# Folding the adaLN partial sums to 64 partitions, with the high part above the low part, before one matmul with ones

## The chip, the cores and the metric

The kernel runs on one core of one Trainium2 chip. The metric is device time in microseconds (us) of one execution. The profile that is read below was taken of one such execution.

## The reference

Two layers of a decoder trunk, 256 tokens wide 1024. Each layer has three sublayers (feed-forward, attention, feed-forward); layer 0's attention is sparse, layer 1's is differential. Every sublayer is wrapped in norms and in a shift, a scale and a gate that come from a conditioning vector `c`:

```
cond = silu(c)
mod = cond @ ada_w[i] + ada_b[i]            # 1024 x 9216 per layer
sh0, sc0, g0, sh1, sc1, g1, sh2, sc2, g2 = split(mod, 9)
h = rmsnorm(x, pre_norm) * (1 + sc) + sh
x = x + (0.5 or 1) * g * rmsnorm(sublayer(h), post_norm)
```

The change is about the 1024-wide pieces of `mod`. All data are float32.

## The kernel before

**Main work.** The two row tiles of x (128 tokens each, t = 0 and 1) go through the six sublayers n = 0 to 5 as two generators that a loop takes turns with. Every weight block is loaded by a DMA on SP's queue into a `raw` tile, then split into a high and a low part: ScalarE (ACT) casts the high part (lines 211 and 234), VectorE (DVE) subtracts it from the raw values to get the low part (lines 212 and 235). TensorE (PE) multiplies high by high, high by low and low by high (lines 267 and 282). Split weights are called `whl` or `wj`; seven such tiles exist. `raw` tiles come from a pool of five buffers, temporary tiles (`tmp`) from a pool of four.

**The modulation vectors.** One piece of `mod` is one call of `ada_items`. Each of the sixteen pieces (all but the shift and scale of sublayer 0, which `first_part` makes) has four items. An item loads 1 MB of `ada_w` (line 307) and adds two products of it into a 128 x 1024 tile `a` with two VectorE instructions (line 311); row p of `a` then holds the partial sum over the eight rows of `ada_w` that lie on partition p. After the fourth item, `end()` adds the 128 partitions up and spreads the sum to all of them: ACT casts `a` to the high part (line 320), DVE subtracts for the low part (line 321), and PE multiplies each half of each part by a matrix of ones (lines 326 and 327: four matmuls of 512 columns, with two in each accumulation). The result `ps_m` is then copied by ACT if the piece is a shift (`sh`, line 329) or combined with a norm weight by DVE if it is a scale or a gate (`g`, `pg`, lines 331 and 333). The norm weight `pnb` is loaded by line 319.

**Order.** `background()` hands out items as the main work goes on, by the table BGCUM: twenty items, so five ends, fall into sublayer 0, and one to four ends into each later one. The ends are called place 1 to place 16 here, in order of time; places 1 to 5 lie between 107 and 221 us, place 6 at 298 us in the sparse attention, place 14 starts at 712 us and is finished in the norm ahead of the differential attention at 735 us. Within an engine the order is laid down by a scheduler when the program is built, and an instruction that waits holds up everything behind it on its engine.

Of the kernel before, what the change touches and what calls it, by code (L numbers as in the profile page):

```python
# [8 lines left out]
F32 = mybir.dt.float32  # L9
F32R = mybir.dt.float32r  # L10
I32 = mybir.dt.int32
AF = mybir.ActivationFunctionType
OP = mybir.AluOpType
# [31 lines left out]
def bcast_rows(ap, n):  # L45
    return bass.AP(tensor=ap.tensor, offset=ap.offset, ap=[[0, 128], [1, n]])
# [3 lines left out]
def trunk(ctx, tc, x, c, positions, ada_w, ada_b, pre_norm, post_norm, ffn_w_gate, ffn_w_up,  # L50
          ffn_w_down, dsa_w_in, dsa_w_out, diff_w_in, diff_w_out, diff_lambda, diff_subln, out):
    nc = tc.nc
    consts = ctx.enter_context(tc.tile_pool(name="consts", bufs=1))
    wpool = ctx.enter_context(tc.tile_pool(name="wpool", bufs=WBUFS))
    rawp = ctx.enter_context(tc.tile_pool(name="rawp", bufs=RAWBUFS))
# [8 lines left out]
    def tmp(name, shape=(128, 1024), dt=F32):  # L64
        return tmpp.tile(list(shape), dt, name=name, tag="tmp")
# [7 lines left out]
    def tr_tile(name):  # L73
        return psum.tile([128, 4, 128], F32, name=name, tag="tr", bufs=2)
# [4 lines left out]
    def half(hf):  # L79
        return slice(hf * 512, (hf + 1) * 512)  # L80

    def flat(t):
        return t.rearrange("p a b -> p (a b)")
# [22 lines left out]
    onesr = consts.tile([128, 128], F32R, name="onesr")  # L106
# [182 lines left out]
    def mod_tile(n, name):  # L289
        MOD.setdefault(n, {})[name] = t = consts.tile([128, D], F32, name=name, tag="mod", bufs=MODBUFS)  # L290
        return t

    def ada_items(n, part):


        l, s = divmod(n, 3)
        c0 = (3 * s + part) * D
        box = {}

        def begin():  # L300
            box["a"] = a = mod_tile(n, ("sh", "g", "pg")[part])
            nc.gpsimd.memset(a, 0.0)
            nc.sync.dma_start(a[0:1, :], ada_b[l:l + 1, c0:c0 + 1024])

        def go(i):
            raw = rawp.tile([128, 2, 1024], F32, name="araw", tag="raw")
            nc.sync.dma_start(raw, ada_w[l, :, c0:c0 + 1024].rearrange("(p j) n -> p j n", j=8)[:, 2 * i:2 * i + 2, :])
            a = box["a"]
            with tc.high_priority(offset=APRI):
                for j in range(2):  # L310
                    nc.vector.scalar_tensor_tensor(a, raw[:, j, :], scond[:, 2 * i + j:2 * i + j + 1], a,  # L311
                                                   op0=OP.mult, op1=OP.add)

        def end():
            a = box["a"]
            hl = rawp.tile([128, 2, 1024], F32R, name="ahl", tag="raw")
            if part:
                pb = tmp("pnb")
                nc.sync.dma_start(pb, bcast_rows((post_norm if part == 2 else pre_norm)[l, s], D))
            nc.scalar.copy(hl[:, 0, :], a)  # L320
            nc.vector.tensor_tensor(hl[:, 1, :], a, hl[:, 0, :].bitcast(F32), op=OP.subtract)
            m = a
            for hf in range(2):
                sl = half(hf)
                ps = tr_tile("ps_m")
                nc.tensor.matmul(flat(ps), onesr, hl[:, 0, sl], start=True, stop=False)
                nc.tensor.matmul(flat(ps), onesr, hl[:, 1, sl], start=False, stop=True)
                if part == 0:
                    nc.scalar.copy(m[:, sl], flat(ps))
                elif part == 1:  # L330
                    nc.vector.scalar_tensor_tensor(m[:, sl], flat(ps), 1.0, pb[:, sl], op0=OP.add, op1=OP.mult)
                else:
                    nc.vector.scalar_tensor_tensor(m[:, sl], flat(ps), 1.0 if s == 1 else 0.5, pb[:, sl],
                                                   op0=OP.mult, op1=OP.mult)

        def item(i):
            if i == 0:
                begin()
            go(i)
            if i == 3:  # L340
                end()

        return [lambda i=i: item(i) for i in range(4)]
# [645 lines left out]
```

## Time and profile before

| | us |
|---|---|
| median of three runs (1059.56 to 1062.03) | 1059.62 |
| the profiled execution's own time | 1058.01 |
| its span in the trace | 1056.2 |
| PE busy in the span | 1015.5 |
| DVE busy | 788.6 |
| ACT busy | 523.8 |

Matmuls overlap one another, so PE's busy time says that it has work, and the distance between two starts says what one matmul takes. [...]

### The profile page before, as it was taken

What the parts mean: (1) busy time and instruction counts of PE and PEld (TensorE: products, weight loads), DVE (VectorE), ACT (ScalarE), POOL (GpSimd) and SP (SyncE); (2) the same over time, 40 slices, a digit from 0 to 9 for tenths busy, and PEclk for the clock granted to TensorE, in tenths of its full rate; (3) what the DMA queues carried; (4) which work ended last, traced back from release to release, by engine and by line L of the source; (5) the groups of instructions that cost most, each with busy time, mean ns of one, the idle gap of its engine ahead of it and who ended that gap; (6) DMA issues with size and microseconds to landing.
All of it is one profiled execution on the core that took longest, in us unless ns stands there. A gap on an engine that the chain in (4) does not pass through costs nothing.

```text
span 1056.2 us, 15311 instructions
## 1 busy us (share of the span) xinstructions
PE 1015.5 (96%) x5936; PEld 873.6 (83%) x5936; DVE 788.6 (75%) x1121; ACT 523.8 (50%) x834; POOL 45.0 (4%) x49
## 2 busy tenths in 40 slices
PE   5999999989999999999999999999999899999997
PEld 2689997769778789998878999887777678999875
DVE  5769887989976977877688967767988575765643
ACT  3354534455575654543455544346477555544432
POOL 1000000001000200000030000001000120000000
PEclk9999999999999999999999999999999999999999
DMA  9959899986443477988757979956653443778431
GB/s 315 343 147 322 313 321 378 347 293 218 148 142 128 155 273 247 352 286 291 271 193 260 314 257 316 316 208 236 260 200 118 153 134 115 243 235 261 183 117 40
DMA packets 93732, 249.48 MB, mean 236 GB/s; under 512 B 6084, under 2 KB 24652, under 8 KB 93660
## 3 DMA queue, kind: packets, MB, share of 16 engines
q1 hardware_dynamic: 93660, 248.52, 68.1%
q8 instruction: 46, 0.75, 0.3%
q14 instruction: 26, 0.21, 0.1%
HBM read 247.44 MB, written 1.05 MB: 235 GB/s over the span
## 4 chain that ended last, share of the span: by engine, by line
PE 57%; issue 20%; DVE 4%; ACT 3%; POOL 2%; DMA 1%; POOLq 0%; DVEq 0%; ACTq 0%
PE ydown L267 15%; PE up L282 9%; PE gate L282 8%; PE gate L267 3%; PE up L267 3%; PE projQd L267 2%; PE projQ L267 2%; PE projV L267 2%; PE projA L267 2%; PE projK L267 2%; PE ydsa L267 1%; POOL rstd L407 1%; DVE whl L235 1%; PE dsaO L752 1%; PE ydiff L267 1%
## 5 line engine op out<-in xcount | busy, mean ns | idle before, releaser
L235 DVE TENSOR_TENSOR whl<-raw,whl 128x1024 fp32r<-128x1024 f32 (+3 forms) x216 | 245.7, 1150 | 98.5 <-ACT whl L234 97.7
L234 ACT CAST whl<-raw 128x1024 fp32r<-128x1024 f32 (+3 forms) x216 | 211.8, 995 | 190.1 <-PE ydown L267 89.5
L282 PE MATMUL gate<-HT,wj 128*128 128x256 f32 x1344 | 166.2, 284 | 1.5 <-DVE wj L212 1.4
L212 DVE TENSOR_TENSOR wj<-raw,wj 128x1024 fp32r<-128x1024 f32 x112 | 134.7, 1221 | 43.1 <-ACT wj L211 42.8
L211 ACT CAST wj<-raw 128x1024 fp32r<-128x1024 f32 x112 | 116.4, 1050 | 100.3 <-DMA raw<-in_ffn_w_up_dram 21.5
L282 PEld LDWEIGHTS gate<-HT,wj 128*128 128x128 f32 x1344 | 163.4, 192 | 2.2 <-DVE wj L212 1.9
L282 PE MATMUL up<-HT,wj 128*128 128x256 f32 x1344 | 164.4, 283 | 0.0
L282 PEld LDWEIGHTS up<-HT,wj 128*128 128x128 f32 x1344 | 162.8, 192 | 0.4
L267 PE MATMUL ydown<-whl,ffj 128*128 128x512 f32 x672 | 157.0, 390 | 2.2 <-DVE whl L235 2.2
L267 PEld LDWEIGHTS ydown<-whl,ffj 128*128 128x128 f32 x672 | 125.7, 188 | 30.6 <-DVE whl L235 3.1
L267 PE MATMUL gate<-whl,HT 128*128 128x480 f32 x384 | 94.3, 392 | 0.4 <-ACT HT L393 0.2
L267 PE MATMUL ydown<-whl,ffa 128*128 128x512 f32 (+1 forms) x368 | 89.3, 393 | 1.9 <-ACT whl L234 1.9
L267 PEld LDWEIGHTS gate<-whl,HT 128*128 128x128 f32 x384 | 72.2, 191 | 16.6 <-ACT HT L393 2.7
L267 PEld LDWEIGHTS ydown<-whl,ffa 128*128 128x128 f32 (+1 forms) x368 | 67.9, 188 | 19.7 <-issue 3.6
L311 DVE SCALAR_TENSOR_TENSOR pg<-araw,scond,pg 128x1024 f32<-128x1024 f32 x48 | 61.4, 1280 | 6.4 <-DMA araw<-in_ada_w_dram 5.8
L267 PE MATMUL up<-whl,HT 128*128 128x480 f32 x288 | 66.0, 381 | 0.0
L267 PEld LDWEIGHTS up<-whl,HT 128*128 128x128 f32 x288 | 53.5, 188 | 8.4 <-ACT sg L512 0.5
L311 DVE SCALAR_TENSOR_TENSOR g<-araw,scond,g 128x1024 f32<-128x1024 f32 x40 | 51.2, 1281 | 7.8 <-DMA araw<-in_ada_w_dram 7.4
L311 DVE SCALAR_TENSOR_TENSOR sh<-araw,scond,sh 128x1024 f32<-128x1024 f32 x40 | 51.2, 1280 | 1.3 <-DMA araw<-in_ada_w_dram 0.8
L468 POOL TENSOR_TENSOR rstdy<-rstdy,mhalf 128x1 f32<-128x1 f32 x12 | 10.2, 850 | 824.2 <-ACT rstdy L467 824.2
L267 PE MATMUL projV<-whl,HT 128*128 128x512 f32 x96 | 28.4, 416 | 0.0
L267 PE MATMUL projQ<-whl,HT 128*128 128x512 f32 x96 | 27.6, 415 | 0.0
(224 smaller groups left out, 1090.7 us busy)
## 6 DMA issues: line engine op xcount, KB each, us to landing
araw<-in_ada_w_dram SPq DMA_DIRECT2D x64, 1024.0 KB
raw<-in_ffn_w_down_dram SPq DMA_DIRECT2D x40, 1024.0 KB
raw<-in_ffn_w_gate_dram SPq DMA_DIRECT2D x56, 512.0 KB
raw<-in_ffn_w_up_dram SPq DMA_DIRECT2D x56, 512.0 KB
raw<-in_ffn_w_gate_dram SPq DMA_DIRECT2D x16, 960.0 KB
raw<-in_diff_w_in_dram SPq DMA_DIRECT2D x12, 1024.0 KB
raw<-in_ffn_w_up_dram SPq DMA_DIRECT2D x12, 960.0 KB
fraw<-in_ada_w_dram SPq DMA_DIRECT2D x32, 256.0 KB
```

Of the source, the lines that this page charges most:

```text
L211: nc.scalar.copy(hl[0], raw)
L212: nc.vector.tensor_tensor(hl[1], raw, hl[0].bitcast(F32), op=OP.subtract)
L234: nc.scalar.copy(hl[:, 0, 0:n], raw[:, j, 0:n])
L235: nc.vector.tensor_tensor(hl[0:r, 1, 0:n], raw[0:r, j, 0:n], hl[0:r, 0, 0:n].bitcast(F32), op=OP.subtract)
L267: nc.tensor.matmul(acc[:, hf, 0:n], lhs, rhs, start=(first and hf not in seen), stop=(last and i % 3 == 2))
L282: nc.tensor.matmul(a[:, b, :], w[:, wp, j, b * 128:(b + 1) * 128], HT[:, :, hp, k0 + j, :], start=(first and j == 0 and i == 0 and b % 2 = ...
L311: nc.vector.scalar_tensor_tensor(a, raw[:, j, :], scond[:, 2 * i + j:2 * i + j + 1], a, op0=OP.mult, op1=OP.add)
L407: nc.gpsimd.tensor_tensor(r, r, mhalf[:, 0:1], op=OP.pow)
L468: nc.gpsimd.tensor_tensor(r, r, mhalf[:, 0:1], op=OP.pow)
L752: nc.tensor.matmul(flat(O)[:, h * 64:(h + 1) * 64], ptb[u][:, i * nb + b, :], v[:, b, :], start=(b == 0), stop=(b == nb - 1), skip_group_c ...
```

## The change

In `end()`, ACT first copies rows 64 to 127 of `a` down to partitions 0 to 63 of a new tile `aup`, and DVE adds rows 0 to 63 to them. The sum of 64 rows is then split: ACT casts it to the high part on partitions 0 to 63 of `ahl`, DVE writes the low part to partitions 64 to 127. One matmul of ones over all 128 partitions then adds high and low at once, so each half takes one matmul in place of two. `aup` lies in the `raw` pool where `ahl` lay before, and `ahl` moves to the `tmp` pool. The load of `pnb` now stands behind the allocation of both tiles.

```diff
         def end():
             a = box["a"]
-            hl = rawp.tile([128, 2, 1024], F32R, name="ahl", tag="raw")
+            up = rawp.tile([128, 2, 1024], F32, name="aup", tag="raw")
+            hl = tmp("ahl", (128, 1024), F32R)
             if part:
                 pb = tmp("pnb")
                 nc.sync.dma_start(pb, bcast_rows((post_norm if part == 2 else pre_norm)[l, s], D))
-            nc.scalar.copy(hl[:, 0, :], a)
-            nc.vector.tensor_tensor(hl[:, 1, :], a, hl[:, 0, :].bitcast(F32), op=OP.subtract)
+            w, f = up[0:64, 0, :], up[0:64, 1, :]
+            nc.scalar.copy(w, a[64:128, :])
+            nc.vector.tensor_tensor(f, a[0:64, :], w, op=OP.add)
+            nc.scalar.copy(hl[0:64, :], f)
+            nc.vector.tensor_tensor(hl[64:128, :], f, hl[0:64, :].bitcast(F32), op=OP.subtract)
             m = a
             for hf in range(2):
                 sl = half(hf)
                 ps = tr_tile("ps_m")
-                nc.tensor.matmul(flat(ps), onesr, hl[:, 0, sl], start=True, stop=False)
-                nc.tensor.matmul(flat(ps), onesr, hl[:, 1, sl], start=False, stop=True)
+                nc.tensor.matmul(flat(ps), onesr, hl[:, sl], start=True, stop=True)
```

Lines 320 and 321 thus become four: 323 (ACT copy), 324 (DVE add), 325 (ACT cast) and 326 (DVE subtract); the matmul is line 331, and every line of the program behind it is 4 higher than before (the cast of a weight stays line 234, the copy of a shift is 333).

The scheduler also lays the order down anew. At place 3, in the down projection of sublayer 0, ACT's order was this (`ahl<-sh` is the high part of the shift's sums, `whl<-raw` the high parts of weights):

```order
L234 CAST whl<-raw 128x1024 x2
L393 CAST ffj<-actj 128x512
L320 CAST ahl<-sh 128x1024
L329 COPY sh<-ps_m 128x512 x2
L234 CAST whl<-raw 128x1024 x8
```

and is now this:

```order
L234 CAST whl<-raw 128x1024 x2
L397 CAST ffj<-actj 128x512
L323 COPY aup<-sh 64x1024
L325 CAST ahl<-aup 64x1024
L333 COPY sh<-ps_m 128x512 x2
L234 CAST whl<-raw 128x1024 x8
```

Both of ACT's steps and the copies of the result stand ahead of the next eight casts of weights.

At place 4, one piece later, DVE's order was this (line 311 makes the partial sums, line 333 the result, line 235 the low parts of weights):

```order
L235 TENSOR_TENSOR whl<-raw,whl 128x1024 x2
L311 SCALAR_TENSOR_TENSOR pg<-araw,scond,pg 128x1024 x2
L321 TENSOR_TENSOR ahl<-pg,ahl 128x1024
L333 SCALAR_TENSOR_TENSOR pg<-ps_m,pnb 128x512 x2
L235 TENSOR_TENSOR whl<-raw,whl 128x1024 x2
```

and is now this:

```order
L235 TENSOR_TENSOR whl<-raw,whl 128x1024 x2
L311 SCALAR_TENSOR_TENSOR pg<-araw,scond,pg 128x1024 x2
L324 TENSOR_TENSOR aup<-pg,aup 64x1024
L326 TENSOR_TENSOR ahl<-aup,ahl 64x1024
L337 SCALAR_TENSOR_TENSOR pg<-ps_m,pnb 128x512 x2
L235 TENSOR_TENSOR whl<-raw,whl 128x1024 x2
```

The add and the subtraction stand one behind the other, with nothing between them for the time in which ACT casts; place 5 reads the same.

At place 14 the subtraction has moved. It stood 20 microseconds ahead of the norm; DVE's order in the norm of t = 0 ahead of the differential attention was this (`h` is the modulated row tile, `HT` the low part of its transpose):

```order
L235 TENSOR_TENSOR whl<-raw,whl 128x1024
L415 SCALAR_TENSOR_TENSOR h<-h,rstd,sh 128x512 x2
L235 TENSOR_TENSOR whl<-raw,whl 128x1024
L394 TENSOR_TENSOR HT<-ps_x,HT 128x512 x2
L470 TENSOR_TENSOR u<-ydown,pg 128x512 x2
```

and is now this:

```order
L235 TENSOR_TENSOR whl<-raw,whl 128x1024
L419 SCALAR_TENSOR_TENSOR h<-h,rstd,sh 128x512 x2
L235 TENSOR_TENSOR whl<-raw,whl 128x1024
L326 TENSOR_TENSOR ahl<-aup,ahl 64x1024
L398 TENSOR_TENSOR HT<-ps_x,HT 128x512 x2
L474 TENSOR_TENSOR u<-ydown,pg 128x512 x2
```

The subtraction now stands between the weights and `HT`.

## Rows read from the trace of the kernel before

**Rows 1.** The page: busy us (share of the span), instructions.
```profile
PE 1015.5 (96%) x5936; PEld 873.6 (83%) x5936; DVE 788.6 (75%) x1121; ACT 523.8 (50%) x834; POOL 45.0 (4%) x49
```
**Rows 2.** Stretches: length, PE, PEld, DVE, ACT, POOL busy (instructions), PE clock, DMA share, GB/s.
```profile
100.00:150.00 50.00, 49.89 (x409) 49.34 (x408) 43.96 (x48) 20.32 (x23) 0.00 (x0) 1.00 0.85 305
...
175.00:200.00 25.00, 24.12 (x104) 18.94 (x103) 23.00 (x21) 10.26 (x11) 0.00 (x0) 1.00 1.00 362
...
600.00:650.00 50.00, 50.00 (x415) 49.83 (x414) 37.43 (x36) 24.49 (x27) 0.00 (x0) 1.00 0.84 283
```
**Rows 3.** Timeline, PE at place 1: start us, us, engine line op tiles.
```profile
114.40 0.39 PE L327 MATMUL ps_m<-ahl,onesr 128*128 128x512 f32 x1
...
114.63 0.39 PE L326 MATMUL ps_m<-ahl,onesr 128*128 128x512 f32 x1
```
**Rows 4.** The tiles `ps_m` and `ahl`: count, ns min/median/max, first and last start.
```profile
L326 PE MATMUL ps_m<-ahl,onesr x32: 390/392/497, 114.2 to 1000.9; 128*128 128x512 f32 x32
...
L320 ACT CAST ahl<-pg x6: 1047/1056/1059, 107.8 to 984.1; 128x1024 fp32r<-128x1024 f32 x6
L321 DVE TENSOR_TENSOR ahl<-pg,ahl x6: 1218/1222/1226, 108.9 to 985.3; 128x1024 fp32r<-128x1024 f32 x6
```
**Rows 5.** Groups of DVE by form: count, busy us, mean ns, idle before.
```profile
L235 DVE TENSOR_TENSOR whl<-raw,whl 64x1024 fp32r<-64x1024 f32 x4 | 4.9, 1216 | 12.5 <-ACT whl L234 12.5
```
**Rows 6.** Timeline, place 2: ACT, DVE and PE (in brackets the idle time before).
```profile
138.68 1.03 ACT L558 ACTIVATE sgj<-gate 128x1024 f32<-128x1024 f32 x1
138.76 1.23 DVE L321 TENSOR_TENSOR ahl<-g,ahl 128x1024 fp32r<-128x1024 f32 x1 [1.16 <-ACT ahl L320]
...
142.29 2.91 PE L282 MATMUL up<-HT,wj 128*128 128x256 f32 x23
```
**Rows 7.** Timeline, place 3.
```profile
168.42 1.05 ACT L320 CAST ahl<-sh 128x1024 fp32r<-128x1024 f32 x1 [2.42 <-DVE sh L311]
169.51 1.23 DVE L321 TENSOR_TENSOR ahl<-sh,ahl 128x1024 fp32r<-128x1024 f32 x1 [1.18 <-ACT ahl L320]
...
171.32 1.07 ACT L329 COPY sh<-ps_m 128x512 f32<-128x512 f32 x2 [1.85 <-PE ps_m L327]
...
172.28 3.90 ACT L234 CAST whl<-raw 128x1024 fp32r<-128x1024 f32 x4
...
173.40 12.90 PE L267 MATMUL ydown<-whl,ffa 128*128 128x512 f32 x54 [1.87 <-ACT whl L234]
```
**Rows 8.** Timeline, place 4.
```profile
193.73 1.22 DVE L321 TENSOR_TENSOR ahl<-pg,ahl 128x1024 fp32r<-128x1024 f32 x1 [1.12 <-ACT ahl L320]
...
195.25 0.64 PE L327 MATMUL ps_m<-ahl,onesr 128*128 128x512 f32 x2
...
195.69 1.29 DVE L333 SCALAR_TENSOR_TENSOR pg<-ps_m,pnb 128x512 f32<-128x512 f32 x2 [0.74 <-PE ps_m L327]
...
196.90 2.35 DVE L235 TENSOR_TENSOR whl<-raw,whl 128x1024 fp32r<-128x1024 f32 x2
...
198.17 21.16 PE L267 MATMUL ydown<-whl,ffj 128*128 128x512 f32 x92 [0.88 <-DVE whl L235]
```
**Rows 9.** Timeline, place 5.
```profile
217.25 1.23 DVE L321 TENSOR_TENSOR ahl<-g,ahl 128x1024 fp32r<-128x1024 f32 x1 [1.12 <-ACT ahl L320]
...
220.07 1.29 DVE L331 SCALAR_TENSOR_TENSOR g<-ps_m,pnb 128x512 f32<-128x512 f32 x2 [1.59 <-PE ps_m L327]
...
222.54 10.28 PE L267 MATMUL ydown<-whl,ffj 128*128 128x512 f32 x44 [1.37 <-DVE whl L235]
```
**Rows 10.** Timeline, place 6 (q is the query of t = 1).
```profile
296.02 1.06 ACT L710 ACTIVATE q<-projQ 128x512 f32<-128x512 f32 x2
...
303.71 0.60 PE L594 MATMUL ps_b<-ident,q 128*128 128x128 f32 x4
```
**Rows 11.** Timeline, the norm ahead of the differential attention.
```profile
733.36 1.79 PE L267 MATMUL projK<-whl,HT 128*128 128x512 f32 x6
733.69 1.28 DVE L394 TENSOR_TENSOR HT<-ps_x,HT 128x512 fp32r<-128x512 f32 x2
```

## The prediction

> **What bounds the kernel now.** I read the page first. PE is busy for 96% of the span, DVE for 75%, ACT for 50% [rows 1]: the kernel looks bound by TensorE, and a change that takes matmuls out looks like a gain. The busy time by stretches says where that holds. Between 600 and 650 us PE is busy for 50.00 of 50 us, DVE for 37 [rows 2]: a microsecond of PE work less there is a microsecond gained, and DVE and ACT have room. Between 175 and 200 us, PE is busy for 24.12 of 25 us, but DVE for 23.00, and the DMA share is 1.00 [rows 2]. Five of the sixteen pieces fall into 100 to 221 us, and there I read the timeline instruction by instruction. PE waits for DVE or ACT behind places 3, 4 and 5: its main matmuls start again 1.87, 0.88 and 1.37 us late, released by weights whose split stood behind the piece's own steps [rows 7 to 9]. Those steps are what the change lengthens.
>
> **What is taken away.** Each end loses two of its four matmuls, 32 of the 64 in all (32 on line 326 [rows 4] and as many on line 327). Two of these matmuls start 0.23 us apart [rows 3], so one end gives PE 0.46 us back, and all sixteen 7.4 us. I count this only where PE is the bound: places 7 to 16, ten times 0.46, so 4.6 us. At places 1 to 6 it is in the times worked out below.
>
> [...]
>
> **What is added.** Per end, one ACT instruction and one DVE instruction of 1024 columns. No row of before shows the copy from partitions 64 to 127 down to 0 to 63, nor a 64-row add. Bounds: half of the 128-row price if rows counted, the full price if columns do. The only 64-row DVE row of this length takes 1.22 us [rows 5], the 128-row one 1.22 too [rows 4], so I take the full price, 1.22 us on DVE and 1.05 on ACT [rows 4]. The chain from the last partial sum to the ones matmul was cast, subtraction; it is now copy, add, cast, subtraction: longer by 1.05 + 1.22 and two hand-overs of about 0.03 (cast ends at 169.47, subtraction starts at 169.51 [rows 7]), so **2.3 us**. Whether that reaches PE is asked place by place.
>
> - *Place 1* (108 us): PE's new order puts the two matmuls behind the first of the main ones that followed them, which covers the chain. Counted at zero.
> - *Place 2* (139 us): ACT's cast now stands behind `sgj`, which ends at 139.71 [rows 6], and needs the add, over at 139.99. Cast to 141.05, subtraction to 142.3, then the two matmuls to 142.8, then a weight's low part, which DVE does after the subtraction, until 143.5. PE's main matmuls began again at 142.29 [rows 6]. Cost 1.2 us; less 0.2 for place 1's matmuls, **1.0**.
> - *Place 3* (168 us): the first order listing shows all steps and the copies of the result ahead of the weights' casts, on which PE waits. Those began at 172.28 and let PE go at 173.40 [rows 7]. The whole chain shifts by 2.3: **+2.3**. PE had nothing else to do.
> - *Place 4* (193 us): in the second listing DVE goes straight from the add to the subtraction and sits idle for ACT's cast. The subtraction ends at 194.95 + 2.33 = 197.28; the result followed the matmul's start by 0.44 (195.25 to 195.69 [rows 8]), so it starts at 197.8 in place of 195.69, and the weights behind it, which release PE at 198.17, come as late: **+2.1**. DVE, with 23.00 of 25 us busy [rows 2], has no room to catch up in.
> - *Place 5* (217 us): the same, but before, DVE waited 1.59 us for PE to come to these matmuls [rows 9], and that wait covers part. Subtraction until 220.8, result at 221.25 in place of 220.07: **+1.2**.
> - *Place 6* (298 us): ACT copies the query of t = 1, at 296.02 before [rows 10], now behind the piece's copy and its cast, and the cast waits for DVE's add. That is about 5 us later, and PE transposes the query at 303.71 [rows 10], so some 4 us were spare; the rest of that attention's softmax chain is late. Between 0 and 3; I take **+1.5**, nearest to the 1 us left plus the filler matmuls that PE's new order no longer has there.
> - *Place 14* (735 us): the subtraction stands ahead of `HT`'s low part (third listing). PE's first six matmuls there already take 1.79 us, 0.4 more than six times 0.23, waiting for it [rows 11]. One DVE instruction: **+1.2**.
> - *Places 7 to 13, 15, 16*: PE does not wait there (50.00 of 50 us busy around place 12 [rows 2]), because weights lie ready ahead of it and the two matmuls stand well behind their subtraction in PE's order; the longer chain is taken to cost nothing. If that cover were gone, each would cost up to 2.3.
>
> `aup` holds a `raw` buffer until its subtraction, up to 1.5 us longer than `ahl` did at places 3 and 4, which delays the next load on SP's queue; the chain's own delay gives that load the same time back, so nothing is added. The `pnb` loads go to later places in SP's queue and are still issued well ahead of their use; counted at zero, at most the wait of one result.
>
> Sum: 1.0 + 2.3 + 2.1 + 1.2 + 1.5 + 1.2 - 4.6 = **+4.7 us**. The profiled execution took 1058.0 us (span 1056.2 and 1.8 around it), which makes 1062.7; the median of the runs, 1059.6, is 1.6 longer than that execution, and the result is told as a median, so I forecast **1064.3**.
>
> DVE starts the second of two weight subtractions before the first has ended (two of 1.22 take 2.35 [rows 8]). [...]
>
> **The rivals.**
> *A: the DMAs set the pace in sublayer 0* and DVE's delays vanish behind them. For it: DMA share 1.00 between 175 and 200 us [rows 2]. Against it: PE's waits there are released by DVE and ACT, not by a load [rows 7 to 9]. It decides if the weights of places 3 to 5 land more than 2 us after their turn on DVE. Then these places cost nothing: 1.0 + 1.5 + 1.2 - 4.6 = -0.9, so 1058.7, no change.
> *B: PE's work decides nearly everywhere*, as its 96% says, and the two added instructions hide in DVE's 25% of idle time. It ends on the other side. The place is sublayer 0 again: weights would have to lie ready more than 2.3 us ahead at places 3 to 5, as they do later on. Then all 7.4 us are gained: 1052.2. Against it stand the three waits of PE [rows 7 to 9]. A half-way case, where place 6 and 14 cost nothing and the early places half, is near 1058.
> *C: the reordered attention stages* lose more than I counted. The new order moves instructions throughout both attentions, where chains of short instructions on three engines set the time. If place 6 costs 3 and place 15, in the differential attention, another 2.3, the time is 1064.3 + 1.5 + 2.3 = 1068.1.
> *D: 64-row instructions cost half.* Then the chain is as long as before, places 2 to 5 cost nothing, and the time is near 1057.7. The row of 64 partitions [rows 5] speaks against it; it has no chance of its own and is counted with A.
>
> **How the numbers follow.** About 0.3%, so 3.2 us, is what a measurement of this kernel can tell from no change. Forecast 0.42 and C 0.12, both slower; A with D and the half-way case 0.28, no change; B, whole or more than half, 0.18, faster. Part of the forecast's own range, 1061.5 to 1067 (place 6 from 0 to 3, place 14 from 0), lies below 1062.8, which moves 0.04 to no change. So slower 0.50, same 0.32, faster 0.18. The range of 1055 to 1069 takes in C and A and leaves out the better half of B.
>
> **What would show it.** Right: PE's main matmuls start 2 us later behind each of places 3, 4 and 5, counted from the last partial sum, with an idle gap of about 1.1 us between the add and the subtraction on DVE; the down projection of sublayer 0 ends some 6 us later than before; from 400 us on the lag shrinks by 0.46 us per place. Lines 324 and 326 take 1.2 us. Wrong: if sublayer 0 ends at the same time as before (A), if the 64-row instructions take 0.6 us (D), or if the lag at 236 us is below 2 us (B).

## The result, and the profile after

The changed kernel takes 1064.39 us (median of 16 runs, 1062.43 to 1067.30) against 1056.98 us for the kernel before (16 runs, 1054.44 to 1062.03): the ratio is 1.0063, with an interval of 1.0052 to 1.0075. The forecast was 1064.3 us, and the sum behind it +4.7 us. Of two profiled executions the one after is longer by 4.4 us (spans of 1060.6 and 1056.2 us).

The page of the changed kernel, to be read beside [rows 1]:

```profile
PE 1010.6 (95%) x5904; PEld 868.7 (82%) x5904; DVE 807.2 (76%) x1137; ACT 539.5 (51%) x850; POOL 42.6 (4%) x49
```

PE has 32 instructions and 4.9 us less to do, DVE 18.6 us more and ACT 15.7 us more, and the span is longer. The tiles give the prices of the new steps (count, ns min/median/max, first and last start):

```profile
L331 PE MATMUL ps_m<-ahl,onesr x32: 387/395/505, 117.8 to 1005.5; 128*128 128x512 f32 x32
L325 ACT CAST ahl<-aup x16: 1030/1045/1053, 115.4 to 994.7; 64x1024 fp32r<-64x1024 f32 x16
L326 DVE TENSOR_TENSOR ahl<-aup,ahl x16: 1218/1219/1221, 116.5 to 996.1; 64x1024 fp32r<-64x1024 f32 x16
...
L323 ACT COPY aup<-pg x6: 1046/1050/1050, 108.8 to 989.0; 64x1024 f32<-64x1024 f32 x6
L324 DVE TENSOR_TENSOR aup<-pg,aup x6: 1209/1218/1220, 109.8 to 990.1; 64x1024 f32<-64x1024 f32 x6
```

Each of these steps on 64 partitions takes as long as one on 128 [rows 4]: 1.05 us on ACT, 1.22 us on DVE. Rival D falls.

**Where the time goes** I read from the lag: the start of the k-th matmul of the main products (lines 267 and 282 of before and of after; both have 5168 of them) in the trace after, less that in the trace before. It is worked out from the two traces and is no view of the profile.

| stretch | lag at its start, us | at its end | cost | forecast |
|---|---|---|---|---|
| places 1 and 2 (110 to 152 us) | 0.15 | 1.32 | +1.2 | +1.0 |
| place 3 (168 to 190) | 1.31 | 5.72 | +4.4 | +2.3 |
| place 4 (190 to 202) | 5.72 | 6.07 | +0.35 | +2.1 |
| place 5 (218 to 232) | 6.07 | 7.38 | +1.3 | +1.2 |
| end of sublayer 0 (232 to 260) | 7.38 | 6.43 | -0.95 | 0 |
| place 6, to the gate of n = 2 (to 375) | 6.43 | 7.24 | +0.8 | +1.5 |
| places 7 to 13 (to 717) | 7.24 | 4.59 | -2.65 | -3.2 |
| place 14 (to 746) | 4.59 | 5.49 | +0.9 | +0.7 |
| places 15 and 16, to the end | 5.49 | 4.44 | -1.05 | -0.9 |

The sum is right, and most rows are. Places 3 and 4 are not: together they cost 4.75 us against 4.4, but nearly all of it at place 3. Its timeline after, beside [rows 7]:

```profile
169.64 1.05 ACT L323 COPY aup<-sh 64x1024 f32<-64x1024 f32 x1 [2.43 <-DVE sh L311]
170.72 1.22 DVE L324 TENSOR_TENSOR aup<-sh,aup 64x1024 f32<-64x1024 f32 x1 [1.17 <-ACT aup L323]
171.97 1.04 ACT L325 CAST ahl<-aup 64x1024 fp32r<-64x1024 f32 x1 [1.28 <-DVE aup L324]
173.05 1.22 DVE L326 TENSOR_TENSOR ahl<-aup,ahl 64x1024 fp32r<-64x1024 f32 x1 [1.11 <-ACT ahl L325]
174.32 0.74 PE L331 MATMUL ps_m<-ahl,onesr 128*128 128x512 f32 x2 [3.13 <-DVE ahl L326]
...
175.82 3.89 ACT L234 CAST whl<-raw 128x1024 fp32r<-128x1024 f32 x4
...
176.93 18.88 PE L267 MATMUL ydown<-whl,ffa 128*128 128x512 f32 x68 [1.87 <-ACT whl L234]
```

The chain goes as forecast: copy, add, cast and subtraction one behind the other, 1.11 us of idle DVE between add and subtraction, and PE's main matmuls back at 176.93 us; the lag there is 3.54, which is 2.23 more than ahead of place 3. But the 68 matmuls that follow take 18.88 us, 0.28 each, where 54 took 12.90 in before [rows 7], 0.24 each. The stretches of after show why (columns as in [rows 2]):

```profile
172.00:174.00 2.00, 0.00 (x0) 0.00 (x0) 0.95 (x1) 1.01 (x1) 0.00 (x0) 1.00 0.90 330
174.00:176.00 2.00, 0.74 (x2) 0.30 (x2) 0.27 (x1) 1.14 (x3) 0.00 (x0) 0.89 0.65 164
176.00:178.00 2.00, 1.07 (x3) 0.89 (x4) 1.09 (x1) 2.00 (x3) 0.00 (x0) 0.50 0.98 342
178.00:180.00 2.00, 2.00 (x6) 1.62 (x5) 2.00 (x3) 1.81 (x3) 0.00 (x0) 0.50 0.78 150
180.00:182.00 2.00, 2.00 (x6) 1.54 (x5) 1.96 (x3) 1.64 (x2) 0.00 (x0) 0.50 0.83 227
182.00:184.00 2.00, 2.00 (x9) 1.60 (x9) 2.00 (x3) 0.37 (x1) 0.00 (x0) 0.91 1.01 406
```

PE waited 3.13 us, did two matmuls and waited 1.87 us; the granted clock fell to 0.50 and stayed there until about 182 us, with 6 matmuls in 2 us in place of the 10 or 11 of before, where one wait of 1.87 us stands here and the clock was 1.00 throughout:

```profile
176.00:178.00 2.00, 2.00 (x11) 1.62 (x10) 1.97 (x2) 0.19 (x1) 0.00 (x0) 1.00 1.02 217
178.00:180.00 2.00, 2.00 (x10) 1.67 (x9) 2.00 (x3) 0.80 (x1) 0.00 (x0) 1.00 1.00 311
```

The lag grew from 3.54 to 5.72: the fall cost 2.2 us.

Place 4 after, beside [rows 8]:

```profile
199.59 1.22 DVE L326 TENSOR_TENSOR ahl<-aup,ahl 64x1024 fp32r<-64x1024 f32 x1 [1.11 <-ACT ahl L325]
201.33 0.64 PE L331 MATMUL ps_m<-ahl,onesr 128*128 128x512 f32 x2
201.77 1.29 DVE L337 SCALAR_TENSOR_TENSOR pg<-ps_m,pnb 128x512 f32<-128x512 f32 x2 [0.95 <-PE ps_m L331]
...
202.97 2.35 DVE L235 TENSOR_TENSOR whl<-raw,whl 128x1024 fp32r<-128x1024 f32 x2
204.24 2.11 PE L267 MATMUL ydown<-whl,ffj 128*128 128x512 f32 x8 [1.34 <-DVE whl L235]
```

DVE's subtraction is 5.86 us later than in before: 3.5 that DVE was late already, and 2.3 of the longer chain. But PE was 5.7 us late by now, so its wait here grew only from 0.88 to 1.34 us, by no more than the two matmuls less give back; most of DVE's delay was no delay for PE. Place 5 goes as forecast:

```profile
225.65 1.22 DVE L326 TENSOR_TENSOR ahl<-aup,ahl 64x1024 fp32r<-64x1024 f32 x1 [1.11 <-ACT ahl L325]
226.92 0.74 PE L331 MATMUL ps_m<-ahl,onesr 128*128 128x512 f32 x2 [1.53 <-DVE ahl L326]
227.46 1.29 DVE L335 SCALAR_TENSOR_TENSOR g<-ps_m,pnb 128x512 f32<-128x512 f32 x2 [0.60 <-PE ps_m L331]
```

The wait of DVE for PE ahead of the result, 1.59 us in [rows 9], is down to 0.60, and PE now waits 1.53 us for DVE. Place 14, beside [rows 11]:

```profile
738.39 1.22 DVE L326 TENSOR_TENSOR ahl<-aup,ahl 64x1024 fp32r<-64x1024 f32 x1
...
739.64 1.29 DVE L398 TENSOR_TENSOR HT<-ps_x,HT 128x512 fp32r<-128x512 f32 x2
...
740.39 0.73 PE L267 MATMUL projK<-whl,HT 128*128 128x512 f32 x2 [1.24 <-DVE HT L398]
```

PE waits 1.24 us for `HT`, which stands behind the subtraction.

The single runs differ with their mean granted clock: of the kernel before, those at 0.997 took 1054.7 to 1056.4 us and those at 0.990 and 0.991 took 1059.3 to 1062.5. The profiled run of before had 0.993; the 16 runs of the changed kernel had 0.987 to 0.991. In the two profiles the clock falls at the same three later places (mean clock 0.91 from 230 to 250 us, 0.93 from 340 to 365 and 0.91 from 825 to 845, in both); one or more of these falls are missing in late_only, p345_only, p345_no_fold and late_plus. So a kernel does not have them in every execution. Probably that is why the medians lie further apart (7.4 us) than the two profiles (4.4 us); since no clock stands beside the 16 runs of before, it is not shown.

A lag against the one profile of before therefore changes where before has a fall that the other run lacks, whatever the edit does there.

### The profile page after: what moved, and what is told of

The parts are those of the page before. It is cut to its first block, busy times and chain, and to the rows that moved or that the text cites. A ratio compares the mean times of both kernels' runs of the same rounds, so it can differ in the third digit from the quotient of the medians.

```text
span 1060.6 us, 15285 instructions
## 1 busy us (share of the span) xinstructions
PE 1010.6 (95%) x5904; PEld 868.7 (82%) x5904; DVE 807.2 (76%) x1137; ACT 539.5 (51%) x850; POOL 42.6 (4%) x49
## 3 DMA queue, kind: packets, MB, share of 16 engines
HBM read 247.44 MB, written 1.05 MB: 234 GB/s over the span
## 4 chain that ended last, share of the span: by engine, by line
PE 61%; issue 20%; DVE 8%; ACT 5%; DMA 3%; POOL 2%; SPq 0%; DVEq 0%; POOLq 0%; ACTq 0%
PE ydown L267 10%; PE gate L282 10%; PE up L282 10%; PE gate L267 5%; PE up L267 4%; PE projQd L267 2%; DVE whl L235 2%; PE projQ L267 2%; PE projV L267 2%; PE projA L267 2%; PE projK L267 2%; PE ydsa L267 1%; DMA araw<-in_ada_w_dram 1%; DMA raw<-in_ffn_w_down_dram 1%; PE ps_mod L381 1%
## 5 line engine op out<-in xcount | busy, mean ns | idle before, releaser
L267 PE MATMUL ydown<-whl,ffa 128*128 128x512 f32 (+1 forms) x368 | 91.9, 402 | 1.9 <-ACT whl L234 1.9
L562 ACT ACTIVATE sgj<-gate 128x1024 f32<-128x1024 f32 (+1 forms) x16 | 14.7, 919 | 29.1 <-PE gate L282 29.1
```

The lines of the kernel that those rows point to most:

```text
L267: nc.tensor.matmul(acc[:, hf, 0:n], lhs, rhs, start=(first and hf not in seen), stop=(last and i % 3 == 2))
L562: nc.scalar.activation(sg, av, AF.Silu)
```

## The experiments

Lags are given as above, each against the kernel before. The first three take the change apart by place, with both versions of `end()` side by side:

```diff
-        def end():
+        def end_old():
...
+        def end_new():
...
+        end = end_new if (n, part) in (...) else end_old
```

**late_only**: the new one at places 7 to 13 and 16.

> The fold at places 7 to 13 and 16 alone; places 1 to 6, 14 and 15 as before. Theory (the longer chain costs where PE waits for it, in sublayer 0 and at places 6 and 14; elsewhere two matmuls less per place are a gain): eight places at 0.46 us, so 3.7 us faster than before, ratio near 0.9965, and in the profile PE's main matmuls run ahead of before by 0.46 us more behind each place from 370 us on. Rival (the new order of instructions as a whole, or the temporary tile that is taken for the split, is what costs): no gain, ratio 1.000 to 1.003.

Measured: 1054.28 us, ratio 0.9968 (0.9949 to 0.9986). The lag falls from +0.98 us at 343 us to -1.87 at the end, but not all of that is matmuls: 0.94 comes between 343 and 375 us, ahead of place 7, where before has a fall of the clock (mean 0.93 from 340 to 365 us) and late_only none (1.00). From 375 us on it is 1.91. In it, a wait for `act` (the activations, which DVE makes) that before does not have takes 1.3 back at 398 us:

```profile
398.74 0.98 PE L523 MATMUL ps_act<-ident,act 128*128 128x128 f32 x7 [1.18 <-DVE act L545]
```

So the eight places give 3.2 us, 0.40 each, where 8 x 0.46 makes 3.7. At these places, where PE is the bound and the chain has cover, the matmuls that were taken out are time that is gained. Runs at the same mean clock say so without the profile: at 0.997, late_only took 1052.0 to 1053.1 us (four runs), before in the same rounds 1055.4 to 1055.8 (five).

**early_only**: the new one at places 1 to 6.

> The fold at places 1 to 6 alone. Theory: the whole loss and none of the gain of the later places, 1.0 + 2.3 + 2.1 + 1.2 and about 0.4 to 1.5 at place 6, so 7 to 8 us slower than before, ratio 1.0066 to 1.0076. Rival (order or temporary tile): a part of the loss, 2 to 4 us. Rival (DMAs set the pace in sublayer 0): no more than 1 us at places 3 to 5, ratio near 1.002.

Measured: 1066.69 us, ratio 1.0086 (1.0070 to 1.0102). The lag rises from 0.3 to 7.6 us at 232 us and is between 8.1 and 8.3 from 408 us to the end, with nothing regained later. The forecast's five terms for these places make 8.1.

**p345_only**: at places 3 to 5.

> The fold at places 3, 4 and 5 alone, the three ends in the down projection of sublayer 0. Theory: 2.3 + 2.1 + 1.2 = 5.6 us slower than before, ratio 1.0053, with PE's main matmuls as late as that when the down projection ends and no change behind it. Rival (DMAs set the pace there): under 1 us. Rival (order or tile, over all sixteen places): three sixteenths of the loss, 1 to 2 us.

Measured: 1065.23 us, ratio 1.0077 (1.0050 to 1.0104). The lag grows by 5.9 us, from -0.2 to 5.6 at 227 us (forecast +5.6), then goes back to 3.7, where the expectation had no change: 0.7 us at the end of sublayer 0, as in the change, and 0.9 between 349 and 375 us, where it lacks the fall of the clock that before has. At place 3 the clock falls here too, for a shorter time:

```profile
174.00:176.00 2.00, 0.46 (x1) 0.47 (x2) 0.48 (x1) 2.00 (x4) 0.00 (x0) 0.77 0.84 299
176.00:178.00 2.00, 2.00 (x6) 1.52 (x6) 2.00 (x3) 2.00 (x3) 0.00 (x0) 0.50 0.93 213
178.00:180.00 2.00, 2.00 (x10) 1.63 (x9) 1.97 (x2) 2.00 (x3) 0.00 (x0) 0.87 0.46 84
```

With the shorter fall the lag grows by 3.1 us at place 3, and by 1.2 at place 4: less at the one, more at the other.

**no_fold**: the change without its two added steps at all sixteen places; rows 64 to 127 of the partial sums are left out.

```diff
-            up = rawp.tile([128, 2, 1024], F32, name="aup", tag="raw")
...
-            w, f = up[0:64, 0, :], up[0:64, 1, :]
-            nc.scalar.copy(w, a[64:128, :])
-            nc.vector.tensor_tensor(f, a[0:64, :], w, op=OP.add)
+            f = a[0:64, :]
```

> As the change, but without the fold: only rows 0 to 63 of the partial sums are split and added up, the sums of rows 64 to 127 are left out. So the chain has two steps of 64 rows, as long as before, with 32 matmuls less. Theory: the copy and the add are the whole loss; without them all sixteen places gain up to 0.46 us, those in sublayer 0 less since PE waits there anyway: 5 to 7.4 us faster than before, ratio 0.993 to 0.995. Rival (order or temporary tile, which stay as in the change): no better than before, ratio 1.000 to 1.005.

Measured: 1067.67 us, ratio 1.0084 (1.0045 to 1.0122): a miss. Sublayer 0 does become faster (the lag goes from +2.4 us at 95 us to -2.3 at 227). But the scheduler laid all later stages down anew as well, and at place 9 it put the subtraction behind a step that waits for a load:

```profile
480.54 1.28 DVE L311 SCALAR_TENSOR_TENSOR pg<-araw,scond,pg 128x1024 f32<-128x1024 f32 x1 [1.90 <-DMA araw<-in_ada_w_dram]
...
484.19 1.22 DVE L323 TENSOR_TENSOR ahl<-sh,ahl 64x1024 fp32r<-64x1024 f32 x1
...
485.46 1.22 PE L328 MATMUL ps_m<-ahl,onesr 128*128 128x512 f32 x2 [5.91 <-DVE ahl L323]
```

PE waits 5.91 us, the clock falls as well (mean 0.57 from 484 to 492 us), and the lag goes from 3.9 to 12.5 us. This kernel cannot price two steps, since its order differs in too much; the next keeps the rest of the program as it was before.

**p345_no_fold**: the same, at places 3 to 5 alone, with the old `end()` elsewhere.

> As the run with the fold at places 3, 4 and 5 alone, but there only rows 0 to 63 are split and added up and the sums of rows 64 to 127 are left out: the chain has two steps again, and two matmuls per place are gone. The order of instructions outside these places stays that of before. Theory (the copy and the add are the loss): no loss at these places, a gain of up to 0.5 us at each, 0 to 1.5 us faster than before, ratio 0.9986 to 1.000. Rival (whatever is new there besides the copy and the add, the temporary tile or the order, costs): slower than before by 2 us or more, ratio above 1.002.

Measured: 1054.30 us, ratio 0.9953 (0.9934 to 0.9971), a miss, but to the better side. The lag goes from 0.55 us ahead of place 3 to -3.2 at 227 us. Against p345_only that is 9.6 us at three places, more than the two steps' 2.3 us each. The timeline at place 3 shows what else is gone:

```profile
168.71 0.34 SPq L226 DMA_DIRECT2D raw<-in_ffn_w_down_dram  x1
169.67 1.05 ACT L234 CAST whl<-raw 128x1024 fp32r<-128x1024 f32 x1
169.85 1.22 DVE L323 TENSOR_TENSOR ahl<-sh,ahl 64x1024 fp32r<-64x1024 f32 x1
171.63 0.64 PE L328 MATMUL ps_m<-ahl,onesr 128*128 128x512 f32 x2
172.07 1.08 ACT L330 COPY sh<-ps_m 128x512 f32<-128x512 f32 x2 [1.35 <-PE ps_m L328]
172.11 14.88 PE L267 MATMUL ydown<-whl,ffa 128*128 128x512 f32 x62
```

ACT casts a weight ahead of the shift's copies, so PE waits neither ahead of the matmuls with ones nor behind them, and the clock stays at 1.00. The run leaves out a fourth thing too: with no `aup`, and `ahl` among the temporary tiles, no `raw` buffer is held, and the next load of a weight is issued at 168.71 us, 2.85 before that of the kernel before (171.56) and 4.20 before that of p345_only (172.91). So the fold is the loss at these places, and neither the temporary tile nor the single matmul is. But what it costs is its own time, the order that the scheduler gives the casts, the clock, and perhaps the buffer; this run does not part the four, and none tries the buffer alone.

**p345_halves**: places 3 to 5 with copy, add, cast and subtraction each cut into two of 512 columns, so that the first half's add runs beside the second half's copy.

```diff
-            nc.scalar.copy(w, a[64:128, :])
-            nc.vector.tensor_tensor(f, a[0:64, :], w, op=OP.add)
+            for hf in range(2):
+                c = half(hf)
+                nc.scalar.copy(w[:, c], a[64:128, c])
+                nc.vector.tensor_tensor(f[:, c], a[0:64, c], w[:, c], op=OP.add)
```

(and likewise for the cast and the subtraction)

> The fold at places 3, 4 and 5 alone, each of its four steps cut into two halves of 512 columns, so that ACT and DVE work at the same time: with 0.59 us for a half on ACT and 0.69 on DVE the last low part is ready 3.4 us after the last partial sum, against 4.6 with whole steps and 2.35 before. DVE's work grows (four times 0.69 against two times 1.22), its idle time goes. Theory (the length of the chain is the price): half of the loss, about 2.5 to 3 us slower than before, ratio 1.0025, and about 2.5 us faster than the fold in whole steps. Rival (DVE's busy time is the price): as slow as the fold in whole steps, ratio 1.005 or more.

Measured: 1064.36 us, ratio 1.0038 (1.0010 to 1.0065). At places 3 to 5 the lag grows by 2.1 us, from 0.57 at 157 to 2.62 at 227, where p345_only has 5.9. The last low part is ready 3.40 us after the last partial sum, as expected, and PE waits 1.10 us ahead of the matmuls with ones at place 3, where p345_only has 3.03; the clock falls there all the same (mean 0.72 from 172 to 184 us), so the 2.1 us are not the chain alone. The interval of the ratio holds both the theory's 1.0025 and the rival's 1.005; it is the lag that speaks for the theory. The profiled run then loses 4.7 us between 283 and 343 us, in the sparse attention, where the mean clock was 0.83 from 310 to 340 us. The same rise and the same clock came in p345_no_fold and late_plus, so they do not come from the halves; whether an execution has them can move it by more than the edit.

**late_plus**: the new `end()` at places 1, 7 to 13, 15 and 16.

> The fold at places 1, 7 to 13, 15 and 16, where the theory has it cost nothing; places 2 to 6 and 14 as before. Theory: two places more than the fold at places 7 to 13 and 16, so 0.9 us more, 4.3 us faster than before, ratio 0.996. Rival (each new order has gains and losses of its own of this size): anywhere from 0.995 to 1.002.

Measured: 1056.09 us, ratio 0.9981 (0.9960 to 1.0002), no better than late_only. Two places more, worth 0.9 us by the forecast, are less than what the clock does to single runs, and the two intervals overlap: these runs do not tell the two kernels apart.

**doubled**: the change with each matmul of ones issued twice, so that there are 64 again and the spread sums are twice as large.

```diff
-                nc.tensor.matmul(flat(ps), onesr, hl[:, sl], start=True, stop=True)
+                nc.tensor.matmul(flat(ps), onesr, hl[:, sl], start=True, stop=False)
+                nc.tensor.matmul(flat(ps), onesr, hl[:, sl], start=False, stop=True)
```

> The change with each ones matmul run twice into the same sum, so that the modulation vectors come out doubled and PE has 32 matmuls more, as many as before the change. Theory: ten places from 370 us on lose their 0.46 us again, and the places in sublayer 0, where PE waits anyway, lose little: 4.6 to 6 us slower than the change, 11 to 13 us slower than before, ratio 1.0104 to 1.0120. Rival (PE's matmuls are hidden and the gain never came): as the change, ratio 1.006.

Measured: 1070.52 us, ratio 1.0101 (1.0072 to 1.0131). The lag goes from 0.4 to 12.3 us, against 0.15 to 4.4 in the change. Up to 375 us 3.4 us of the difference arise, where the clock falls at other times in the two (doubled has a fall at 201 us and none at 175), so this part prices no matmul. From 375 us on the lag grows by 1.3 us in place of falling by 2.8: 4.1 us for the 20 matmuls of the ten later places, 0.21 each, where the theory had 4.6. So the rival falls.

**fill_three** and **fill_four**: the change with three or four float32 matmuls of no use put on PE at place 3, to keep it busy while it waits.

```diff
+                if (n, part) == (1, 0) and hf == 0:
+                    for _ in range(3):
+                        nc.tensor.matmul(flat(ps), ones, a[:, sl], start=True, stop=True)
                 nc.tensor.matmul(flat(ps), onesr, hl[:, sl], start=True, stop=True)
```

> The change, with three float32 matmuls of no use put into PE's wait at place 3. They read the shift's partial sums and ones, and their result is overwritten by the matmul with ones; ACT's and DVE's orders stay as in the change. In the change PE waits 3.13 us there, then 1.87 us more, and the granted clock is 0.50 from about 175.5 to 182 us, over which PE's lag behind the kernel before grows from 3.54 to 5.72 us. Theory: that wait makes the clock fall, and the 2.2 us it costs lie beside place 4, where DVE is only 3.5 us late, so that place 4 costs nothing in the change. Then the clock stays at 1.00 between 170 and 190 us, the lag at 190 us is about 3.5, place 4 costs up to 2 again, and the lag at 211 us is 5.3 to 6.1 (6.07 in the change): the ratio to the kernel before is 1.0050 to 1.0063. First rival: the clock loss simply adds; the lag at 211 us is 3.9 and the ratio 1.0042. Second rival: the clock falls there whatever PE does; the stretch at 0.50 is the same and so are lag and ratio (1.0063).

Measured with three: 1062.54 us, ratio 1.0052 (1.0030 to 1.0075). The timeline and the stretches of place 3 (the trace shows each of the three as two):

```profile
169.70 2.73 PE L333 MATMUL ps_m<-sh,ones 128*128 128x512 f32 x6
...
174.24 0.74 PE L334 MATMUL ps_m<-ahl,onesr 128*128 128x512 f32 x2 [0.42 <-DVE ahl L326]
176.85 3.37 PE L267 MATMUL ydown<-whl,ffa 128*128 128x512 f32 x12 [1.87 <-ACT whl L234]
```

```profile
174.00:176.00 2.00, 0.74 (x2) 0.30 (x2) 0.19 (x1) 1.21 (x3) 0.00 (x0) 1.00 0.39 72
176.00:178.00 2.00, 1.15 (x4) 0.67 (x4) 1.17 (x2) 2.00 (x3) 0.00 (x0) 1.00 0.96 348
178.00:180.00 2.00, 1.94 (x9) 1.58 (x9) 2.00 (x3) 2.00 (x3) 0.00 (x0) 1.00 0.53 123
```

PE's first wait is 0.42 us in place of 3.13, the second is 1.87 as before, and the clock stays at 1.00. The lag is 1.34 us ahead of place 3, 3.45 behind it (+2.1), and 5.63 behind place 4 (+2.2). So with the clock held, both places cost what the prediction gave them, 2.3 and 2.1, and the end of the two is 0.44 us from that of the change. The theory holds on all its numbers, in one traced execution. The first rival (3.9 at 211 us) and the second (the same clock whatever PE does) fall by the trace; the ratio alone would not tell them apart.

> The same with four such matmuls; by the new order ACT also does one cast of a weight ahead of the two copies of the shift at place 3, so that DVE has a low part to make and PE a weight to go on with right behind the two matmuls with ones. Theory: besides the clock, the second wait of 1.87 us at place 3 goes, for this wait is set by the copies' place ahead of the casts and not by the chain itself; the lag at 190 us is 1.5 to 3.5, at 211 us 3 to 5, and the ratio 1.0035 to 1.0055. Rival: the casts' place is of no matter, since DVE's chain sets the pace; then it is as with three, with 5.3 or more at 211 us.

Measured with four: 1064.57 us, ratio 1.0065 (1.0046 to 1.0084): the ratio misses, and so does the lag at 211 us, 7.25 against 3 to 5. At place 3 it goes as the theory says and further: the lag is 3.75 us ahead of it and 3.75 behind it, at 177 us, since the cast ahead of the copies gives PE a weight to go on with. But at place 4 PE waits 2.61 us for DVE, the lag jumps from 3.65 to 7.25, and the clock is at 0.83 between 200 and 210 us: the wait and the fall have moved one place on. (1.4 us of the lag came at 20 to 30 us, ahead of every place, with a fall of the clock of its own.)

## Why the prediction was right

The forecast of 1064.3 us, slower, came true, and the sum of +4.7 stands beside 4.4 in the profiles.

- *What is taken away*: 0.46 us for each late place. Right: 2.65 of 3.2 us at places 7 to 13, 0.40 us a place in late_only, and early_only, which keeps their old version, regains nothing there. For one such matmul doubled has 0.21 us at the later places, where the prediction took 0.23.
- *What is added*: the full price of 1.22 and 1.05 us for 64 rows and a chain 2.3 us longer. Right to 0.1 us at places 3 to 5. The load that waits for `aup` at place 3 goes out at 174.29 us in place of 171.56; whether that costs anything, as the prediction denies, no run tries.
- *Place 3 and place 4* are the steps that failed, each by 2 us in opposite directions. The prediction has no term for a fall of PE's clock (1.00 in [rows 2]) and added the two places up. In fact PE's clock fell after its longer wait at place 3; the 2.2 us lost by that gave DVE a lead of the same size, which paid for place 4. fill_three shows both: no fall, and the two terms as forecast. That the sum was hit within 0.4 us is luck in one thing, that a fall's cost was near the chain's.
- *Place 5* and *places 1 and 2*: right within 0.2 us. The sign that the prediction named (PE back 2 us later at each of places 3 to 5, counted from the last partial sum) came at places 3 and 4 (2.3 and 2.5 us) and not at 5 (1.3), where its own term is 1.2: sign and term did not agree.
- *Place 6*: +0.8 where 1.5 was taken, within its bounds of 0 to 3. The mechanism is there: ACT copies the query 11.42 us later than before (307.44 us), 5.0 more than the lag, and PE transposes it 7.7 us later. The 0.95 us that PE regained at the end of sublayer 0 were not in the sum. Of them, 0.68 are a shorter wait for the modulated row tile `h`, 2.71 us after and 3.39 before:

```profile
236.22 1.77 PE L418 MATMUL ps_x<-ident,h 128*128 128x128 f32 x8 [3.39 <-DVE h L415]
...
242.91 1.60 PE L422 MATMUL ps_x<-ident,h 128*128 128x128 f32 x8 [2.71 <-DVE h L419]
```

- *Place 14*: right, by one DVE instruction ahead of `HT`. No run tries this place alone.
- *The base* was off: the three runs shown had a median of 1059.62 us, and 16 runs 1056.98. The sum was too small by about as much (4.7 against 7.4 us between medians), probably because more of the changed kernel's runs are at a lower clock. The two errors hide each other in the 1064.3, and that is luck too.
- *The range* of 1061.5 to 1067 for the forecast: its stated terms (place 6 from 0 to 3, place 14 from 0) give 1061.6 to 1065.8, so the upper end does not follow from them.

Rival A falls, since PE was late by DVE's chain at places 2, 3 and 5, and at place 4 too where the clock held (fill_three). Rival B was wrong for the early places and right for the late ones: late_only, the version that does the change only where B's condition holds, beats both kernels. Rival C's place 15 gave no loss: places 15 and 16 together regained 1.05 us. Rival D falls by the tiles.

## What to carry to other kernels

Price a change stage by stage: the same edit lost 7.8 us where PE waits for the chain behind a piece and gained some 3 where it does not, and the best of these kernels that compute the whole sum are those that make it only in the second kind. Before adding a step to a chain that PE waits for, ask how long PE will stand still, since a wait can cost its own length and then the clock (here 2.2 us behind waits of 3.13 and 1.87); and do not add such losses up over neighbouring places, as a delay of PE can be a lead for the engine that it will wait for next (here place 4 cost 0.35 us in place of 2.1). A re-laid order can move more than the edit (in no_fold the lag rose by 8.6 us at place 9): an experiment on one step should leave the other stages as they were.

## What was not expected of the hardware

- After a wait of 3.13 us and one of 1.87 with two matmuls between, the granted clock stood at 0.50 until about 182 us, some 5 us after work had begun again; with 0.42 and 1.87 us (fill_three) it stayed at 1.00. The length of the waits alone does not tell: behind 1.10 and 1.62 us (p345_halves, place 3, where PE was idle for 2.82 of the 6 us from 170 us) it fell, to 0.50 between 174 and 178 us, and behind 1.58 and 1.35 us (fill_three, place 4) it did not.
- In the trace of the changed kernel 916 DVE instructions start less than 0.06 us after the end of the one ahead, or before it; 789 of them start before it, by 0.08 us in the median (counted from the trace). Line 326, the new subtraction, never does, nor does an instruction behind it. The timeline of the changed kernel at places 10 and 8, and of the kernel before at place 8:

```profile
510.19 1.22 DVE L324 TENSOR_TENSOR aup<-pg,aup 64x1024 f32<-64x1024 f32 x1
511.33 1.21 DVE L235 TENSOR_TENSOR whl<-raw,whl 128x1024 fp32r<-128x1024 f32 x1
...
430.46 1.22 DVE L212 TENSOR_TENSOR wj<-raw,wj 128x1024 fp32r<-128x1024 f32 x1
431.71 1.22 DVE L326 TENSOR_TENSOR ahl<-aup,ahl 64x1024 fp32r<-64x1024 f32 x1
432.96 1.28 DVE L311 SCALAR_TENSOR_TENSOR sh<-araw,scond,sh 128x1024 f32<-128x1024 f32 x1
...
417.97 1.23 DVE L321 TENSOR_TENSOR ahl<-g,ahl 128x1024 fp32r<-128x1024 f32 x1 [1.11 <-ACT ahl L320]
419.11 2.35 DVE L212 TENSOR_TENSOR wj<-raw,wj 128x1024 fp32r<-128x1024 f32 x2
```

The weight's subtraction starts 1.14 us behind the add, before that has ended, and so does the one behind the old subtraction, line 321. Line 326 starts 1.25 us behind the one ahead of it, and its successor 1.25 behind it, each after the end of the other, though the cast that line 326 needs had ended 1.0 us before. Against the 1.14 us that is 0.11 us each time. Line 326 writes from partition 64; no run lets it write elsewhere, so whether that is the reason is not shown. Between add and subtraction at places 3 to 5 the 1.11 us of waiting for ACT cover it.
